# Scaling tokens by expert weights: a three-token load moved from behind the first input tile to behind the third, and one token's product moved from ScalarE to VectorE

## The chip, the core and the metric

The kernel runs on one core of a Trainium2 chip. The metric is the device time of one execution in microseconds (us). Before the change it is 240.13 us, the median of three runs that lie between 239.79 and 240.28 us.

## The reference, cut to what matters

```python
batch, seq, hidden, n_experts = 16, 1024, 512, 8
k = 2
x_expanded = x[:, :, np.newaxis, :].repeat(k, axis=2)
weights = expert_weights[..., np.newaxis]
return (x_expanded * weights).astype(np.float32)
```

Each of 16,384 tokens has a row of 512 float32 values and two weights. The output holds the row twice, each copy multiplied by one weight. The expert indices are not used. Input rows are 33.55 MB, the output is 67.11 MB, and the weights are 0.13 MB. There is no arithmetic beyond one multiplication per output value.

## The kernel before, in words

128 partitions hold 128 tokens each. They are cut into five **tiles** of 25 tokens per partition (`groups`, L32) and a rest of three (`LAST`, L34); 5 x 25 + 3 = 128. Within a tile the 25 rows of a partition lie one behind another in memory, so a tile's load is one row of 25 x 2 KB = 50 KB per partition.

- **Loads** are issued from ScalarE (its DMA queue is q10 in the profile). Two input tiles fit in memory at a time (`x_pool`, two buffers, L44). `load(i)` (L68) issues tile i; tile 0 is loaded in two steps of 9 and 16 tokens (`FIRST`, L35). Behind tile 0, still inside `load(0)`, stands the load of the last three tokens into a tile of its own, `z_tile` (L84 and L85). Tiles 0 and 1 are loaded at the start (L154); tile i + 2 is issued when tile i has been used up (L159), since it takes the same buffer. On ScalarE's queue the order is thus: tile 0 (9 tokens), tile 0 (16), the three tokens, tile 1, then tile 0's products on ScalarE, tile 2, and so on.
- **Weights** are loaded by SyncE (queue q1) in three pieces between the two steps of tile 0: those of tile 0 (L95), of tiles 1 to 4 (L97), and of the last three tokens (L104). A partition of each piece is 200 bytes (four times 200 for the middle piece) or 24 bytes long.
- **Products** go into one output ring, `o_ring`, that has room for one tile, 25 tokens of 1024 values (L48). Each tile is cut into chunks: two of 13 and 12 tokens for tiles 0 and 1, three of 9, 8 and 8 for the later tiles (L157). `SHARES` (L36) says how many tokens of a chunk VectorE computes: it takes them four at a time (L127, `CH` = 4), and ScalarE takes the remaining tokens of the chunk, two activations for each (L117). A chunk of a tile can be written to the ring only when the output transfer of the chunk that lay there before has landed.
- **Stores** are issued from SyncE, queue q1, one per chunk (L152), behind the weights on the same queue. The last one is the store of the three tokens, whose product VectorE makes in one instruction at the end (L160).

The framework puts in all waits on semaphores; the order of the instructions on each engine is that of the program.

Of the kernel before, what the change touches and what calls it, by code (L numbers as in the profile page):

```python
# [1 line left out]

# [4 lines left out]


@with_exitstack
def kernel(  # L10
    ctx: ExitStack,
    tc: tile.TileContext,
    x: bass.AP,
    expert_indices: bass.AP,
    expert_weights: bass.AP,
    out: bass.AP,
):
    nc = tc.nc

    batch, seq, hidden = x.shape  # L20
    k = expert_weights.shape[-1]
    P = nc.NUM_PARTITIONS
    ntok = batch * seq
    assert ntok % P == 0
    A_TOTAL = ntok // P

    f32 = mybir.dt.float32
    row = k * hidden
    CH = 4


    groups = [25, 25, 25, 25, 25]  # L32
    TX = max(groups)
    LAST = 3  # L34
    FIRST = [9, 16]  # L35
    SHARES = [[9, 8], [9, 8], [9, 8, 8]]  # L36
    assert sum(groups) + LAST == A_TOTAL

    xf = x.rearrange("b s h -> (b s) h")
    of = out.rearrange("b s k h -> (b s) (k h)")  # L40
    wf = expert_weights.rearrange("b s k -> (b s) k")

    w_pool = ctx.enter_context(tc.tile_pool(name="w_pool", bufs=1))
    x_pool = ctx.enter_context(tc.tile_pool(name="x_pool", bufs=2))  # L44
    o_pool = ctx.enter_context(tc.tile_pool(name="o_pool", bufs=1))

    w_tile = w_pool.tile([P, A_TOTAL * k], f32)
    o_ring = o_pool.tile([P, TX * row], f32)  # L48

    def rows(of_all, done, T):  # L50
        return of_all[done * P : (done + T) * P, :].rearrange(
            "(p a) n -> p (a n)", a=T
        )


    if LAST:
        z_pool = ctx.enter_context(tc.tile_pool(name="z_pool", bufs=1))
        z_tile = z_pool.tile([P, LAST * hidden], f32)

    tiles = []  # L60
    done = 0
    for n in groups:
        tiles.append((done, n))
        done += n

    loaded = []

    def load(i):  # L68
        if i >= len(tiles):
            return  # L70
        done, n = tiles[i]
        x_tile = x_pool.tile([P, TX * hidden], f32)
        src = rows(xf, done, n)
        steps = FIRST if i == 0 else [n]
        for e, step in enumerate(steps):
            at = sum(steps[:e])
            nc.scalar.dma_start(
                out=x_tile[:, at * hidden : (at + step) * hidden],
                in_=src[:, at * hidden : (at + step) * hidden],
            )  # L80
            if i == 0 and e == 0:
                for g in range(3):
                    weights(g)
        if i == 0 and LAST:  # L84
            nc.scalar.dma_start(out=z_tile, in_=rows(xf, A_TOTAL - LAST, LAST))  # L85
        loaded.append(x_tile)


    T0 = groups[0]
    G = len([n for n in groups[1:] if n == T0])  # L90
    head = (1 + G) * T0

    def weights(e):
        if e == 0:
            nc.sync.dma_start(out=w_tile[:, : T0 * k], in_=rows(wf, 0, T0))  # L95
        elif e == 1:
            nc.sync.dma_start(  # L97
                out=w_tile[:, T0 * k : head * k].rearrange("p (g n) -> p g n", g=G),
                in_=wf[T0 * P : head * P, :].rearrange(
                    "(g p a) n -> p g (a n)", g=G, p=P  # L100
                ),
            )
        else:
            nc.sync.dma_start(  # L104
                out=w_tile[:, head * k :], in_=rows(wf, head, A_TOTAL - head)
            )

    def product(engine, o_tile, t, x_in, c, m):

        o = t * row  # L110
        if engine is not None:
            for e in range(m * k):
                out_e = o_tile[:, o + e * hidden : o + (e + 1) * hidden]
                in_e = x_in[:, e // k * hidden : (e // k + 1) * hidden]
                w_e = w_tile[:, c + e : c + e + 1]
                if engine is nc.scalar or engine is nc.any and (c + e) % 3 == 2:
                    nc.scalar.mul(out=out_e, in_=in_e, mul=w_e)  # L117
                else:
                    nc.vector.tensor_scalar(
                        out=out_e,  # L120
                        in0=in_e,
                        scalar1=w_e,
                        scalar2=None,
                        op0=mybir.AluOpType.mult,
                    )
            return
        nc.vector.tensor_tensor(  # L127
            out=o_tile[:, o : o + m * row].rearrange(
                "p (t k h) -> p t k h", t=m, k=k
            ),  # L130
            in0=x_in[:, : m * hidden]
            .rearrange("p (t h) -> p t h", t=m)
            .unsqueeze(2)
            .to_broadcast([P, m, k, hidden]),
            in1=w_tile[:, c : c + m * k]
            .rearrange("p (t k) -> p t k", t=m)
            .unsqueeze(3)
            .to_broadcast([P, m, k, hidden]),
            op=mybir.AluOpType.mult,
        )  # L140

    def fill(o_tile, x_in, c, m, v):
        for t in range(0, v, CH):
            u = min(t + CH, v)
            product(None, o_tile, t, x_in[:, t * hidden : u * hidden], c + t * k, u - t)
        product(nc.scalar, o_tile, v, x_in[:, v * hidden :], c + v * k, m - v)

    def emit(src, dst, c, cuts, shares):
        for at, to, v in zip(cuts, cuts[1:], shares):
            o_tile = o_ring[:, at * row : to * row]  # L150
            fill(o_tile, src[:, at * hidden : to * hidden], c + at * k, to - at, v)
            nc.sync.dma_start(out=dst[:, at * row : to * row], in_=o_tile)  # L152

    for i in range(2):  # L154
        load(i)
    for i, (done, n) in enumerate(tiles):
        cuts = [0, 13, n] if i < 2 else [0, 9, 17, n]  # L157
        emit(loaded[i], rows(of, done, n), done * k, cuts, SHARES[min(i, 2)])
        load(i + 2)  # L159
    emit(  # L160
        z_tile,
        rows(of, A_TOTAL - LAST, LAST),
        (A_TOTAL - LAST) * k,
        [0, LAST],
        [LAST],
    )

# [1 line left out]
_INS = ['x', 'expert_indices', 'expert_weights']  # L169
_OUTS = [((16, 1024, 2, 512), 'float32')]  # L170


# [23 lines left out]
```

## Time and profile before

| what | value |
| --- | --- |
| median of three runs | 240.13 us (239.79 to 240.28) |
| the profiled execution: its time, its span | 240.12 us, 238.3 us |
| VectorE busy | 122.6 us, 51% of the span |
| ScalarE busy | 21.2 us, 9% of the span |
| bytes moved by DMA | 100.80 MB |

The span runs from the first to the last instruction that the profiler saw. The profiled execution's own time is 1.8 us longer than its span, and 0.01 us from the median. Every transfer is spread over 16 DMA engines, which work for both queues, q10 (loads) and q1 (weights and stores). A transfer consists of packets; here one packet is mostly one partition's row of the transfer.

### The profile page before, as it was taken

To read this page: it belongs to the slowest core of one execution; us is meant where nothing else is said; L and a number is where in the kernel's file an instruction comes from. 1 tells how busy PE (TensorE), PEld (TensorE's weight loads), DVE (VectorE), ACT (ScalarE), POOL (GpSimd) and SP (SyncE) were. 2 spreads that over 40 slices of the span, in tenths; PEclk is the share of its full clock that TensorE was granted. 3 is DMA by queue.
4 is the path that set the end of the run, shared out by engine and by line. 5 is a ranking of instruction groups with operands and counts; after the bars stand their busy time and mean duration, and the time that the engine had idled before them with its cause. 6 is when DMAs were issued, how large, how long until landed. Compare 5 with 4: busy or idle time off the path is not lost.

```text
span 238.3 us, 167 instructions
## 1 busy us (share of the span) xinstructions
DVE 122.6 (51%) x32; ACT 21.2 (9%) x33; POOL 0.2 (0%) x4
## 2 busy tenths in 40 slices
DVE  0599600000069292099405999493086999865000
ACT  0008900000061250000000000000000000000000
POOL 0000000000000000000000000000000000000000
DMA  7999999999999999999999999999999999999996
GB/s 264 465 386 504 457 414 413 413 424 429 429 396 429 472 465 426 422 404 405 412 484 431 402 434 444 414 434 425 449 408 461 434 440 431 421 413 423 440 434 264
DMA packets 3840, 100.80 MB, mean 423 GB/s; under 512 B 1152, under 2 KB 1152, under 8 KB 1280
## 3 DMA queue, kind: packets, MB, share of 16 engines
q1 hardware_dynamic: 2832, 67.24, 65.5%
q10 hardware_dynamic: 1008, 33.55, 33.2%
HBM read 33.69 MB, written 67.11 MB: 423 GB/s over the span
## 4 chain that ended last, share of the span: by engine, by line
DMA 58%; DVE 28%; issue 2%; another core or an unknown queue 2%; ACT 1%; DVEq 0%; SPq 0%
DMA out_dram<-o_ring 55%; DVE o_ring L127 28%; DMA x_tile<-in_x_dram 3%; ACT o_ring L117 1%; DVEq L127 0%; SPq L152 0%
## 5 line engine op out<-in xcount | busy, mean ns | idle before, releaser
L127 DVE TENSOR_TENSOR o_ring<-x_tile,w_tile 128x4096 f32<-128x4096 f32 (+1 forms) x31 | 119.3, 3905 | 93.2 <-DMA out_dram<-o_ring 82.3
L117 ACT ACTIVATE o_ring<-x_tile,w_tile 128x512 f32<-128x512 f32 x32 | 19.9, 708 | 47.1 <-DMA out_dram<-o_ring 47.0
L127 DVE TENSOR_TENSOR o_ring<-z_tile,w_tile 128x3072 f32<-128x3072 f32 x1 | 3.4, 3359 | 2.1 <-DMA out_dram<-o_ring 2.1
L117 ACT ACT_TABLE_LOAD x1 | 1.3, 1283 | 18.7 <-DMA x_tile<-in_x_dram 18.7
L180 POOL MEMSET const-uint8-127<- 128x1 uint8 x1 | 0.1, 102 | 0.0
L180 POOL MEMSET const-bfloat16-1.0<- 128x1 bf16 x1 | 0.1, 101 | 0.0
L180 POOL MEMSET const-float32-0.0<- 128x1 f32 x1 | 0.1, 98 | 0.2 <-issue 0.2
L180 POOL MEMSET const-float32-1.0<- 128x1 f32 x1 | 0.1, 98 | 0.0
## 6 DMA issues: line engine op xcount, KB each, us to landing
x_tile<-in_x_dram ACTq DMA_DIRECT2D x4, 6400.0 KB, 31.6
out_dram<-o_ring SPq DMA_DIRECT2D x6, 4096.0 KB, 21.5
out_dram<-o_ring SPq DMA_DIRECT2D x3, 4608.0 KB, 27.3
out_dram<-o_ring SPq DMA_DIRECT2D x2, 6656.0 KB, 33.1
out_dram<-o_ring SPq DMA_DIRECT2D x2, 6144.0 KB, 44.5
x_tile<-in_x_dram ACTq DMA_DIRECT2D x1, 4096.0 KB, 17.5
x_tile<-in_x_dram ACTq DMA_DIRECT2D x1, 2304.0 KB, 8.1
out_dram<-o_ring SPq DMA_DIRECT2D x1, 1536.0 KB, 19.5
```

What stands on the lines that cost most here:

```text
L117: nc.scalar.mul(out=out_e, in_=in_e, mul=w_e)
L127: nc.vector.tensor_tensor(out=o_tile[:, o : o + m * row].rearrange("p (t k h) -> p t k h", t=m, k=k), in0=x_in[:, : m * hidden] .rearrange ...
L180: nc = _bacc.Bacc("TRN2", target_bir_lowering=False, num_devices=1)
```

## The change

The changed kernel makes three edits.

- The load of `z_tile` is taken out of `load(0)` and put at the end of `load(2)`, behind the load of tile 2 on ScalarE's queue.
- Ahead of tile 2's load, ScalarE copies one element per partition from the very end of the output ring into `z_tile`. That element belongs to tile 0's last product on ScalarE, so the copy runs behind that product; and as the load of `z_tile` overwrites what the copy wrote, it waits for the copy.
- In tile 0's second chunk (12 tokens), VectorE computes nine tokens in place of eight, and ScalarE three in place of four. On VectorE this adds one instruction of 128 x 1024 values (as two groups of four and one token); on ScalarE it removes two activations of 128 x 512.

```diff
-    SHARES = [[9, 8], [9, 8], [9, 8, 8]]
+    SHARES = [[9, 9], [9, 8], [9, 8, 8]]
...
         x_tile = x_pool.tile([P, TX * hidden], f32)
         src = rows(xf, done, n)
         steps = FIRST if i == 0 else [n]
+        if i == 2 and LAST:
+            nc.scalar.copy(out=z_tile[:, :1], in_=o_ring[:, TX * row - 1 :])
         for e, step in enumerate(steps):
...
-        if i == 0 and LAST:
+        if i == 2 and LAST:
             nc.scalar.dma_start(out=z_tile, in_=rows(xf, A_TOTAL - LAST, LAST))
         loaded.append(x_tile)
```

The order on ScalarE is then: tile 0 (9 tokens), tile 0 (16), tile 1, 14 activations of tile 0, the copy, tile 2, the three tokens, tile 1's activations, and so on as before. Bytes, number of transfers and the order on SyncE are the same.

## The prediction

> **What bounds the kernel now.** I read the page first, for its engines and queues, and then the busy time by stretches.
>
> ```profile
> DVE 122.6 (51%) x32; ACT 21.2 (9%) x33; POOL 0.2 (0%) x4
> ...
> DMA  7999999999999999999999999999999999999996
> ...
> DMA packets 3840, 100.80 MB, mean 423 GB/s; under 512 B 1152, under 2 KB 1152, under 8 KB 1280
> ...
> q1 hardware_dynamic: 2832, 67.24, 65.5%
> q10 hardware_dynamic: 1008, 33.55, 33.2%
> ```
>
> The two queues' packets fill 65.5 + 33.2 = 98.7% of the time of 16 DMA engines. Only 1.3% of 238.3 us, 3.1 us, is idle. Where it lies, the stretches tell (DMA share and GB/s are the last two columns):
>
> ```profile
> 0.00:2.00 2.00, 0.00 (x0) 0.00 (x0) 0.20 (x4) 1.00 0.21 41
> 2.00:25.07 23.07, 16.24 (x5) 6.32 (x10) 0.00 (x0) 1.00 1.01 426
> 25.07:51.90 26.83, 2.38 (x1) 4.87 (x8) 0.00 (x0) 1.00 1.02 430
> 51.90:67.50 15.60, 0.00 (x0) 0.00 (x0) 0.00 (x0) 1.00 1.00 433
> 67.50:82.00 14.50, 9.90 (x3) 5.02 (x9) 0.00 (x0) 1.00 1.01 438
> 82.00:100.00 18.00, 8.76 (x2) 4.99 (x8) 0.00 (x0) 1.00 0.98 422
> 100.00:128.00 28.00, 14.30 (x5) 0.00 (x0) 0.00 (x0) 1.00 0.99 425
> 128.00:218.00 90.00, 71.05 (x18) 0.00 (x0) 0.00 (x0) 1.00 1.00 432
> 218.00:236.50 18.50, 0.00 (x0) 0.00 (x0) 0.00 (x0) 1.00 0.98 423
> 236.50:238.30 1.80, 0.00 (x0) 0.00 (x0) 0.00 (x0) 1.00 0.02 7
> ```
>
> The first 2 us miss 0.79 x 2.0 = 1.6 us and the last 1.8 us miss all but 2%, 1.76 us; together 3.3, so the whole idle time. (Shares over 1.00 come from packets counted whole in the stretch in which they start.) From 2.0 to 236.5 us no stretch lies below 0.98. **The bound is the transport of 100.80 MB**, and its rate hardly depends on what is moved: 426 and 430 GB/s for the loads at the start, 433 for stores alone.
>
> The chain of waits names VectorE for 28%, but that is only the partner in a ring: a product waits for a store to land, and the next store waits for the product, while the other chunk's store fills the engines.
>
> **What the change touches.** These are the first transfers, from the list of issues in narrow windows (the column after the size is us from issue to landing), with the instructions around them:
>
> ```profile
> z_tile<-in_x_dram ACTq DMA_DIRECT2D x1, 768.0 KB, 19.1
> x_tile<-in_x_dram ACTq DMA_DIRECT2D x1, 6400.0 KB, 33.8
> x_tile<-in_x_dram ACTq DMA_DIRECT2D x1, 6400.0 KB, 21.8
> w_tile<-in_expert_weights_dram SPq DMA_DIRECT2D x1, 100.0 KB, 36.7
> w_tile<-in_expert_weights_dram SPq DMA_DIRECT2D x1, 3.0 KB, 50.3
> 1.17 0.42 SPq L97 DMA_DIRECT2D w_tile<-in_expert_weights_dram  x1
> 1.64 0.50 SPq L104 DMA_DIRECT2D w_tile<-in_expert_weights_dram  x1
> 1.64 0.52 ACTq L85 DMA_DIRECT2D z_tile<-in_x_dram  x1
> 2.19 0.81 ACTq L77 DMA_DIRECT2D x_tile<-in_x_dram  x1
> 8.83 18.62 DVE L127 TENSOR_TENSOR o_ring<-x_tile,w_tile 128x4096 f32<-128x4096 f32 x5 [8.83 <-DMA x_tile<-in_x_dram]
> 20.03 9.91 ACT L117 ACTIVATE o_ring<-x_tile,w_tile 128x512 f32<-128x512 f32 x16
> 29.97 0.37 ACTq L77 DMA_DIRECT2D x_tile<-in_x_dram  x1
> 25.07 42.40 DMA out_dram<-o_ring
> ```
>
> So the three tokens land at 1.64 + 19.1 = 20.7 us, tile 1 at 36.0, tile 2 at 29.97 + 21.8 = 51.8, the middle weights at 37.9 and the last weights, 3 KB issued at 1.64, only at 51.9. The first store is issued at 25.07 and lands at 67.47, though its 6.82 MB (6656 KB) take only 15.7 us at 433 GB/s: it does not begin before some 51.8 us. Why a store should stand still for 26 us, the packets between 30 and 49 us show:
>
> ```profile
> q10 hardware_dynamic: 176, 8.19, 103.0%
> q1 hardware_dynamic: 176, 0.01, 0.7%
> ```
>
> Each queue gave 176 packets: the engines take **one packet of each queue in turn**. A weight packet is 200 or 24 bytes, a load packet 50 KB. While loads stand in q10, the weights in q1 advance by one packet for each load packet, and the first store stands behind the weights. Per engine (128 partitions / 16) the weights are 8 + 32 + 8 = 48 packets, and the five loads ahead of tile 3 are 5 x 8 = 40. So the opening is one burst of loads until about 51.8 us, and then stores alone.
>
> **The change, part by part.**
>
> *The load of the three tokens, 786 KB.* Its 8 packets per engine leave the place ahead of tile 1 and come behind tile 2, in the same burst. At 428 GB/s (the mean of the two rows from 2.00 to 51.90) they take 1.84 us. Tile 1 lands at 34.2, tile 2 at 50.0, the three tokens at 51.8, and the burst ends where it ended: the packets ahead of the first store are the same in number and size, and so are their turns with the weights. Term: 0. What comes early is waited for by nobody: VectorE and ScalarE take up tile 1 when the first store has landed, not when the tile has:
>
> ```profile
> 67.57 5.01 ACT L117 ACTIVATE o_ring<-x_tile,w_tile 128x512 f32<-128x512 f32 x8 [37.63 <-DMA out_dram<-o_ring]
> 67.59 9.90 DVE L127 TENSOR_TENSOR o_ring<-x_tile,w_tile 128x4096 f32<-128x4096 f32 x3 [40.13 <-DMA out_dram<-o_ring]
> 77.55 0.33 SPq L152 DMA_DIRECT2D out_dram<-o_ring  x1
> 214.61 3.36 DVE L127 TENSOR_TENSOR o_ring<-z_tile,w_tile 128x3072 f32<-128x3072 f32 x1 [2.11 <-DMA out_dram<-o_ring]
> ```
>
> What comes late has room: the middle weights lose eight turns and land near 50 us instead of 37.9, needed at 67.59; the three tokens land at 51.8, needed at 214.61. On q1 nothing changes its place.
>
> *The shares of tile 0.* VectorE gets one more 128x1024 instruction, ScalarE two activations less:
>
> ```profile
> L127 DVE TENSOR_TENSOR o_ring<-x_tile,w_tile 128x1024 f32<-128x1024 f32 x5 | 6.1, 1219 | 0.0
> L117 ACT ACTIVATE o_ring<-x_tile,w_tile 128x512 f32<-128x512 f32 x32 | 19.9, 708 | 47.1 <-DMA out_dram<-o_ring 47.0
> L180 POOL MEMSET const-float32-1.0<- 128x1 f32 x1 | 0.1, 98 | 0.0
> ```
>
> VectorE ends tile 0 at 8.83 + 18.62 + 1.22 = 28.7 us. ScalarE's 16 activations take 9.91 us, 0.62 each in a row; 14 take 8.67 and end at 28.7. The second store is issued at about 28.8 in place of 29.97, but it queues behind the first, which lands at 67.47. Term: 0.
>
> *The copy.* No row shows a one-element copy on ScalarE. Its bounds are 0.1 us (a 128x1 memset on GpSimd) and 0.71 us (an activation of 512 elements on ScalarE itself); by size it is nearest to the memset, by engine to the activation, and I take 0.3. It waits for the activation ahead of it, and behind it on ScalarE stand tile 2's load, the three tokens' load and tile 1's activations. Tile 2's load is thus issued at 29.0 (28.8 to 29.5), which is 1.0 us earlier than before (0.5 to 1.2), and the three tokens' load some 0.4 us behind it. q10 holds work until tile 1 has passed, at 34.2, so tile 2 is 5 us ahead of its turn: the copy is covered, and would cost only from about 5 us on. Term: 0.
>
> *The handover from loads to stores.* Before, the last load packet of each engine is 50 KB long (1.9 us at 27 GB/s, a sixteenth of 430); after, it is 6 KB (0.23 us). No row shows this handover with short packets. From below: if the change took away every loss in the opening, 2.00 to 51.90 would run at 433 GB/s, and that saves 23.07 x 7/433 + 26.83 x 3/433 = 0.56 us. From above: if the first store had to be fetched after the loads ended, as the very first load was, that costs the 1.6 us of the first row. The nearest row is that of the same short load inside the burst before, 2.00 to 25.07 with a share of 1.01: its eight short packets, between two long loads, left no hole. I take 0.
>
> *Sum.* 240.12 + 0 + 0 + 0 + 0 = 240.12 us for the profiled execution, and as this stands 0.01 us from the median, I forecast **240.1 us**: no change. 0.2%, 0.48 us, is about what a measurement of this kernel can tell from none.
>
> **The rivals.**
>
> *The handover gets shorter* (faster). A hole that long last packets cause goes when the last packets are short. It gives at most the 0.56 us above: 239.5 us. For it: the opening is the place with the lowest rate among the long read stretches, 426. Against it: 2.00 to 25.07, where most of that loss lies, does not change.
>
> *The handover gets longer* (slower). The fetch of the first store is hidden behind the load packets ahead of it, 1.9 us long before and eight of 0.23 us after, and a restart shows. The full price is 1.6 us: 241.7 us. It decides from about 0.5 us of uncovered fetch on. Against it stands the short load before, ahead of tile 1's first packet, with no hole. The Trainium skill, page "DMA: Bandwidth & Descriptors", section "Latency and other measured facts", gives about 0.6 us from issue to first byte on these queues; by that the rival would end at 240.7 us. The trace's first load shows more: the share of 0.21 in the first 2 us.
>
> *The read queue runs dry ahead of tile 2* (slower). It needs tile 2's issue at 34.2 us or later, so a copy of more than 5 us, or one that waits for a store. It would let the first store begin early and mix loads with stores, at the 422 to 425 GB/s of 82 to 128 us; for the 21.4 MB from 2 to 51.9 us moved at 422 in place of 428, 0.7 us: 240.8 us. The order on ScalarE speaks against it: the copy reads what ScalarE itself wrote just before.
>
> *The change does not do what it says*: the held-back load goes early all the same, or lands late but unneeded. Then it is 240.1 us too.
>
> **How the numbers follow.** Forecast, no change: 0.68 (239.7 to 240.5, the spread of the three runs, 0.25 us to either side, and some of the bounds). Not done as said, same time: 0.02. Shorter handover: 0.16. Longer handover: 0.10. Read queue dry: 0.04. So faster by over 0.2% 0.16, within 0.2% 0.70, slower 0.14. The range takes in the shorter handover and the lower part of the longer one, by half its price: 239.4 to 240.8; left out is most of the longer handover, about 1 in 10, and a little at either end.
>
> **What would show it.** Right: the burst of loads ends and the first store lands at 67.5 within 0.3 us; tile 2's load is issued near 29.0; the DMA share stays at 0.98 or more from 2 to 236.5; the middle weights land near 50 us. Wrong: a landing of the first store later or earlier by 0.5 us or more with the rest shifted along (a handover), a store's packets ahead of 49 us (the read queue dry), or a share below 0.98 in a stretch behind 67.5, which would mean a wait that I have not seen. What no term of mine covers is a change in the rate itself at equal work, as between 422 and 438 among the stretches.

## The result, and the profile after

The changed kernel takes 239.84 us, the median of 16 runs (239.57 to 240.09), beside 240.28 us for 16 runs of the kernel before. The ratio is 0.9981 with a 95% interval of 0.9972 to 0.9990: 0.44 us less, just inside what the prediction called no change. A ratio leaves out runs over 1.5% above the fastest of the same kernel, while a median takes in every run. Measured again later, the changed kernel gave 0.9990 (0.9978 to 1.0002) and, with a wider copy that delays only the three tokens' load, by 0.1 us, 0.9976 (0.9964 to 0.9988). All of its runs and those of the wider copy, 38 in number, lie between 239.49 and 240.28 us. Of 117 runs of the kernel before the fastest is as fast, 239.47, but 26 lie above 240.4, up to 241.13. The change takes away slow outliers more than it speeds up the best execution.

From the page of the changed kernel: the engines, the DMA packets and the two queues.

```profile
DVE 123.8 (52%) x33; ACT 20.2 (8%) x32; POOL 0.2 (0%) x4
...
DMA packets 3840, 100.80 MB, mean 424 GB/s; under 512 B 1152, under 2 KB 1152, under 8 KB 1280
...
q1 hardware_dynamic: 2832, 67.24, 65.7%
q10 hardware_dynamic: 1008, 33.55, 33.2%
```

The same bytes in the same packets fill 98.9% of a span of 237.9 us. VectorE has the one instruction more, ScalarE lost two activations and gained the copy. Busy time by stretches, DMA share and GB/s last:

```profile
2.00:25.07 23.07, 16.02 (x5) 6.08 (x9) 0.00 (x0) 1.00 1.00 425
25.07:51.90 26.83, 3.75 (x2) 4.07 (x8) 0.00 (x0) 1.00 1.03 429
51.90:67.50 15.60, 0.00 (x0) 0.00 (x0) 0.00 (x0) 1.00 1.00 434
67.50:82.00 14.50, 9.90 (x3) 5.01 (x8) 0.00 (x0) 1.00 1.01 438
82.00:100.00 18.00, 8.76 (x2) 5.01 (x8) 0.00 (x0) 1.00 0.97 422
100.00:128.00 28.00, 14.57 (x5) 0.00 (x0) 0.00 (x0) 1.00 0.98 423
128.00:218.00 90.00, 70.77 (x18) 0.00 (x0) 0.00 (x0) 1.00 1.00 433
218.00:236.50 18.50, 0.00 (x0) 0.00 (x0) 0.00 (x0) 1.00 0.98 423
```

No stretch moved by more than 2 GB/s: transport still bounds the kernel. The prediction named a share below 0.98 behind 67.5 us as a sign of a wait that it had not seen; 82 to 100 us now has 0.97, but it moves the same 422 GB/s as before. The instructions around the change, from the timeline, and the landings from the list of issues in narrow windows (tile 1, tile 2, the three tokens, the middle weights, the last weights):

```profile
1.63 0.52 ACTq L79 DMA_DIRECT2D x_tile<-in_x_dram  x1
9.05 19.77 DVE L129 TENSOR_TENSOR o_ring<-x_tile,w_tile 128x4096 f32<-128x4096 f32 x6 [9.05 <-DMA x_tile<-in_x_dram]
28.98 0.19 ACT L76 COPY z_tile<-o_ring 128x1 f32<-128x1 f32 x1
29.05 0.34 ACTq L79 DMA_DIRECT2D x_tile<-in_x_dram  x1
29.43 0.46 ACTq L87 DMA_DIRECT2D z_tile<-in_x_dram  x1
67.83 9.90 DVE L129 TENSOR_TENSOR o_ring<-x_tile,w_tile 128x4096 f32<-128x4096 f32 x3 [39.01 <-DMA out_dram<-o_ring]
127.66 22.90 DVE L129 TENSOR_TENSOR o_ring<-x_tile,w_tile 128x4096 f32<-128x4096 f32 x6 [11.69 <-DMA out_dram<-o_ring]
214.16 3.36 DVE L129 TENSOR_TENSOR o_ring<-z_tile,w_tile 128x3072 f32<-128x3072 f32 x1 [2.13 <-DMA out_dram<-o_ring]
```

```profile
x_tile<-in_x_dram ACTq DMA_DIRECT2D x1, 6400.0 KB, 32.6
x_tile<-in_x_dram ACTq DMA_DIRECT2D x1, 6400.0 KB, 20.4
z_tile<-in_x_dram ACTq DMA_DIRECT2D x1, 768.0 KB, 30.2
w_tile<-in_expert_weights_dram SPq DMA_DIRECT2D x1, 100.0 KB, 48.6
w_tile<-in_expert_weights_dram SPq DMA_DIRECT2D x1, 3.0 KB, 50.5
```

Tile 1 lands at 1.63 + 32.6 = 34.2 us, tile 2 at 49.5, the middle weights at 1.15 + 48.6 = 49.8 and the last ones at 52.1. The opening is the forecast one. The execution starts 0.22 us late (first product at 9.05 in place of 8.83), and tile 1's first product starts 0.24 us late (67.83 for 67.59): the handover from loads to stores costs the same. In these two executions the gain comes behind it. The first instruction that waits for the second chunk of tile 1 to be stored starts at 127.66; the same row of the kernel before:

```profile
127.93 22.90 DVE L127 TENSOR_TENSOR o_ring<-x_tile,w_tile 128x4096 f32<-128x4096 f32 x6 [12.15 <-DMA out_dram<-o_ring]
```

So 0.24 us late has become 0.27 us early, a gain of 0.5 us between 67 and 128 us, where tile 3's load takes turns with stores; at the last product it is 0.45 us (214.16 for 214.61). Two more profiles with the changed order of loads repeat this stretch, but not the total. From tile 1's first product to this row it is 59.83 us here, 59.78 in a second profile of the changed kernel and 59.75 with the wider copy, beside 60.34 and 60.55 in two profiles of the kernel before. Yet the execution of that second profile took 240.20 us.

At the end, one of 16 engines at work all through a window counts as 0.06 of the share, and a window counts a packet where it begins. The kernel before

```profile
236.00:236.50 0.50, 0.00 (x0) 0.00 (x0) 0.00 (x0) 1.00 0.42 172
236.50:237.00 0.50, 0.00 (x0) 0.00 (x0) 0.00 (x0) 1.00 0.06 25
```

has one engine that begins another packet past 236.5 us, and the changed kernel has none:

```profile
236.00:236.50 0.50, 0.00 (x0) 0.00 (x0) 0.00 (x0) 1.00 0.24 98
236.50:237.00 0.50, 0.00 (x0) 0.00 (x0) 0.00 (x0) 1.00 0.00 0
```

This is no mark of the change: the second profile of the changed kernel has a share of 0.12 there, two engines, and so has the second profile of the kernel before.

### The profile page after: what moved, and what is told of

Its sections match the earlier page's. It is cut to its first block, busy times and chain, and to the rows that moved or that the text cites. A ratio compares the mean times of both kernels' runs of the same rounds, so it can differ in the third digit from the quotient of the medians.

```text
span 237.9 us, 167 instructions
## 1 busy us (share of the span) xinstructions
DVE 123.8 (52%) x33; ACT 20.2 (8%) x32; POOL 0.2 (0%) x4
## 4 chain that ended last, share of the span: by engine, by line
DMA 68%; DVE 18%; ACT 3%; issue 2%; ACTq 0%; DVEq 0%; SPq 0%
DMA out_dram<-o_ring 60%; DVE o_ring L129 18%; DMA x_tile<-in_x_dram 7%; ACT o_ring L119 2%; ACT L119 1%; ACTq L79 0%; DVEq L129 0%; SPq L154 0%; ACTq L119 0%
## 5 line engine op out<-in xcount | busy, mean ns | idle before, releaser
L119 ACT ACTIVATE o_ring<-x_tile,w_tile 128x512 f32<-128x512 f32 x30 | 18.7, 708 | 48.1 <-DMA out_dram<-o_ring 48.0
## 6 DMA issues: line engine op xcount, KB each, us to landing
x_tile<-in_x_dram ACTq DMA_DIRECT2D x4, 6400.0 KB, 30.5
out_dram<-o_ring SPq DMA_DIRECT2D x2, 6656.0 KB, 33.1
```

## The experiments

Two things were open: which edit makes the small gain, and whether each edit is really worth nothing by itself. **Theory 1**: the place of the three tokens' load makes the gain, by short last packets at the handover. **Rival**: the share and the earlier issue of tile 2, or scatter. A third, the **theory of the lead**, arose from the first four experiments. Each edit is shown against the kernel that its heading names, the kernel before or the changed one.

**The kernel before, against itself.** No edit.

> The kernel before itself, run a second time as if it were a changed one. Every theory expects a ratio of 1.000; its interval tells how much of the 0.9981 of the changed kernel could be chance. If the median comes out 0.4 us or more from that of the kernel before, the theory that the difference is only scatter gains.

240.06 us (12 runs), ratio 1.0003 (0.9992 to 1.0014). So 0.1% either way is scatter.

**The new share alone, in the kernel before.**

```diff
-    SHARES = [[9, 8], [9, 8], [9, 8, 8]]
+    SHARES = [[9, 9], [9, 8], [9, 8, 8]]
```

> Only the share of tile 0's second chunk (nine tokens on VectorE in place of eight), the load of the three tokens stays behind tile 0. Theory 1 (the place of the three tokens' load, the last and short load ahead of the first store, makes the difference): no change against the kernel before, 240.2 to 240.4 us. Rival (tile 2 is issued 1 us earlier, and that makes it): 239.8 to 239.9 us, a ratio of 0.998.

239.92 us (11 runs, 239.69 to 240.64), ratio 1.0002 (0.9992 to 1.0012). By the ratio the share alone gives nothing.

**The changed kernel with the old share: only the moved load and the copy.**

```diff
-    SHARES = [[9, 9], [9, 8], [9, 8, 8]]
+    SHARES = [[9, 8], [9, 8], [9, 8, 8]]
```

> The load of the three tokens behind tile 2 with the one-element copy, but the old share (eight tokens on VectorE). Theory 1 (place of the load): 239.8 to 239.9 us, a ratio of 0.998. Rival (the share and the earlier issue of tile 2): 240.2 to 240.4 us, a ratio of 1.000.

243.97 us (6 runs, 241.07 to 245.74), ratio 1.0104 (1.0058 to 1.0150). Neither theory had this. Without the new share the move costs 1.0% by the ratio, and 1.6% by the medians (243.97 beside 240.12). The timeline of this kernel, and the packets of both queues between 30 and 48 us (count, MB, share):

```profile
30.03 0.19 ACT L76 COPY z_tile<-o_ring 128x1 f32<-128x1 f32 x1
30.09 0.34 ACTq L79 DMA_DIRECT2D x_tile<-in_x_dram  x1
```

```profile
q10 hardware_dynamic: 99, 4.25, 60.2%
q1 hardware_dynamic: 406, 3.13, 41.1%
```

In the changed kernel, the same window:

```profile
q10 hardware_dynamic: 160, 7.37, 95.0%
q1 hardware_dynamic: 166, 0.03, 0.9%
```

Tile 2's load is issued only 1.04 us later than in the changed kernel, 4.1 us ahead of the 34.2 us at which tile 1 lands there; and still it comes too late. The read queue is empty, the weights rush through, and 3.1 MB of the first store slip in among the loads: the rival "the read queue runs dry", with a point that decides between 29.05 and 30.09 us and not at 34.2.

The packets of tile 1 itself show the late load, too. Its 16 last packets, one on each engine, begin between 31.05 and 31.8 us in both kernels. These are the load packets that begin between 30.5 and 32.5 us, first in the changed kernel, then in this one:

```profile
q10 hardware_dynamic: 16, 0.82, 94.8%
q10 hardware_dynamic: 16, 0.82, 145.3%
```

Of a window of 2 us, 94.8% is 1.9 us for a packet, and 145.3% is 2.9 us. The packet that ought to hide the fetch of tile 2 is itself slower by 1 us; why, no run shows, and the DMA share does not tell, since a slow packet counts as busy. In the changed kernel these packets begin 2.0 us and more after tile 2's load is issued, here only 1.0 to 1.7 us after it.

At the end, this kernel has two engines (0.12) that go on when the others are done, and one of them (0.06) goes on still longer, past 240.5 us:

```profile
237.50:238.00 0.50, 0.00 (x0) 0.00 (x0) 0.00 (x0) 1.00 0.30 123
238.00:238.50 0.50, 0.00 (x0) 0.00 (x0) 0.00 (x0) 1.00 0.12 49
239.00:239.50 0.50, 0.00 (x0) 0.00 (x0) 0.00 (x0) 1.00 0.12 49
239.50:240.00 0.50, 0.00 (x0) 0.00 (x0) 0.00 (x0) 1.00 0.06 25
240.50:241.00 0.50, 0.00 (x0) 0.00 (x0) 0.00 (x0) 1.00 0.06 25
```

**The changed kernel without the copy.**

```diff
-        if i == 2 and LAST:
-            nc.scalar.copy(out=z_tile[:, :1], in_=o_ring[:, TX * row - 1 :])
```

> The changed kernel without the one-element copy. The framework then issues the three tokens' load ahead of tile 2's, so it lies in the middle of the burst of loads, and the last packets ahead of the first store are 50 KB long as before the change. Theory 1 (a short last load at the handover makes the difference): 240.2 to 240.4 us, as before the change. Rival (the three tokens' load only has to leave the head of the queue, ahead of tile 1): 239.8 to 239.9 us.

239.98 us (11 runs, 239.75 to 240.31), ratio 0.9990 (0.9981 to 0.9999): between the two, and not told apart. The timeline shows what the copy is for: without it the load is issued at 21.36 us, in the midst of tile 0's activations and ahead of tile 2's load.

From here on **the theory of the lead**: tile 2's load must be issued some 4 to 5 us ahead of its turn, or the first store gets among the loads. The expectations count the lead to the end of tile 1's packets, which they put at 33.5 to 34 us; below I count it to tile 1's landing, for which there are rows.

**The changed kernel again, and with a wider copy.** The second kernel copies 512 elements per partition.

```diff
-            nc.scalar.copy(out=z_tile[:, :1], in_=o_ring[:, TX * row - 1 :])
+            nc.scalar.copy(out=z_tile[:, :hidden], in_=o_ring[:, TX * row - hidden :])
```

> The changed kernel once more, beside the kernel before on the same chip, with more runs. Theory 1 (a small gain of its own, from the order of the loads): a ratio near 0.998 again, about 239.7 to 239.9 us. Rival (scatter): a ratio of 1.000, within the 0.1% that the kernel before showed against itself.

> The changed kernel with a copy of 512 elements per partition in place of one; it holds tile 2's load back by some 0.5 us more, so that it is issued at about 29.5 us, between the changed kernel (29.05, on time) and the kernel with the old share (30.09, 1% slower). Theory of the lead (tile 2's load must be issued some 4.5 us ahead of the end of tile 1's packets, or the first store slips in among the loads): at the edge, so between 239.8 and 244 us, and more scattered than the changed kernel; the packets of q1 between 30 and 48 us tell which way each went. Rival (the old share is slow for another reason, on VectorE or ScalarE): 239.8 to 239.9 us.

240.03 us and 239.72 us (11 runs each), ratios 0.9990 and 0.9976 as given above. The wider copy missed its purpose: it runs from 28.86 to 29.48 us, but tile 2's load is issued at 28.93, since that load does not wait for a copy into another tile. Only the three tokens' load moved, to 29.51.

**Tile 2 late in the kernel before.** Here the copies go into tile 2's own buffer, so that its load has to wait for them.

```diff
+        if i == 2:
+            for d in range(3):
+                nc.scalar.copy(
+                    out=x_tile[:, d * hidden : (d + 1) * hidden],
+                    in_=o_ring[:, TX * row - hidden :],
+                )
```

> The kernel before, its three tokens' load at its old place, with three copies of 512 elements into tile 2's buffer ahead of tile 2's load; they hold that load back by about 1.9 us, to 31.9 us, where tile 1's packets end at about 35.6. The lead is then 3.7 us, as short as in the kernel with the old share (30.09 against 34). Theory of the lead: 1% slower, 242 to 245 us, and some 3 MB on q1 between 30 and 48 us. Rival (only the moved short load, its late place or the copy's semaphore, makes the old share slow): 240.1 to 240.3 us, and 0.01 MB on q1.

241.67 us (12 runs, 240.10 to 244.70), ratio 1.0051 (1.0025 to 1.0076). The three tokens lie at their old place, the share is the old one, and the kernel is slow all the same once tile 2's load comes at 31.75 us, 4.3 us ahead of the 36.0 us at which tile 1 lands in the kernel before. The profiled execution, 240.26 us, is one of the faster; it has 1.08 MB of the store among the loads:

```profile
q10 hardware_dynamic: 140, 6.35, 84.1%
q1 hardware_dynamic: 198, 1.08, 14.3%
```

So part of the engines took the load in time and part did not. Tile 1's 16 last packets, which begin between 33.1 and 33.75 us, tell the same: of the 2 us from 32.5 they fill 105.4%, where all in time give 94.8% and all late gave 145.3%. That a late tile 2 slows the kernel is thus shown without the moved load and without the new share; the forecast of a full 1% was too high.

**The kernel before, with the weights on the other queue.**

```diff
-                for g in range(3):
-                    weights(g)
+                weights(0, nc.sync)
...
+        if i == 1:
+            for g in range(1, 3):
+                weights(g, nc.scalar)
...
-    def weights(e):
+    def weights(e, queue):
...
```

> The kernel before, with the weights of tiles 1 to 4 and of the last three tokens loaded on ScalarE's queue behind tile 1, so that nothing stands ahead of the first store on SyncE's queue but tile 0's weights. Both theories expect the first store to begin at about 26 us in place of 51 and to take turns with the loads of tiles 1 and 2. Theory of the mixture (loads and stores in turn move fewer bytes per second and drive the 16 engines apart): 242 to 245 us, as in the kernel with the old share. Rival (only the bytes count, whatever their order): 240.1 to 240.3 us.

241.21 us (9 runs, 240.77 to 241.82), ratio 1.0044 (1.0029 to 1.0059). The first store now lands 27.2 us after its issue in place of 42.4, and between 30 and 48 us

```profile
q1 hardware_dynamic: 109, 5.80, 74.5%
q10 hardware_dynamic: 96, 2.46, 31.7%
```

stores and loads share the engines. This shows that the weights at the head of q1 are what holds the first store back in the kernel before. The price is 0.4%, not 1%, but what it is made of is not shown, for the edit brings a second delay: the moved weights now land so late that tile 1's first product waits for them and not for the store:

```profile
67.76 18.57 DVE L129 TENSOR_TENSOR o_ring<-x_tile,w_tile 128x4096 f32<-128x4096 f32 x5 [40.19 <-DMA w_tile<-in_expert_weights_dram]
```

**The changed kernel with a late tile 2.**

```diff
-            nc.scalar.copy(out=z_tile[:, :1], in_=o_ring[:, TX * row - 1 :])
+            for d in range(2):
+                nc.scalar.copy(
+                    out=x_tile[:, d * hidden : (d + 1) * hidden],
+                    in_=o_ring[:, TX * row - hidden :],
+                )
+            nc.scalar.copy(out=z_tile[:, :1], in_=x_tile[:, 2 * hidden - 1 : 2 * hidden])
```

> The changed kernel, new share and all, but with two copies of 512 elements into tile 2's buffer ahead of tile 2's load, which must wait for them: issued at about 30.4 us in place of 29.05, a lead of 3.2 us ahead of the end of tile 1's packets (33.6) in place of 4.6. Theory of the lead (about 4 us are needed): 243 to 246 us, as with the old share (lead 3.4), and 2 to 3 MB on q1 between 30 and 48 us. Rival (the old share itself is what was slow, the lead only scatters): 239.7 to 240.5 us and 0.03 MB on q1.

Tile 2's load is issued at 30.18 us, 4.0 us ahead of 34.2. The 12 runs fall into two heaps: six from 239.75 to 240.12 us, six from 243.64 to 250.02. The ratio, 0.9997 (0.9978 to 1.0016), speaks of the first heap alone; the median of all 12 is 241.88. The profiled execution is of the first heap, at 239.75 us, and has the store fully among the loads:

```profile
q10 hardware_dynamic: 95, 4.04, 56.5%
q1 hardware_dynamic: 416, 3.45, 45.2%
```

So the new share does not protect from a store among the loads. Of the 12 runs with the lead gone, half lie 4 to 10 us above the other half, and none of the 38 runs with the lead in place does. A store among the loads need not cost anything, else this execution would be slow too; what makes one execution lose 4 us and another none is open, and there is no profile of the second heap.

**The changed kernel with the old share and the lead given back.** The three tokens are loaded twice, early and late.

```diff
-    SHARES = [[9, 9], [9, 8], [9, 8, 8]]
+    SHARES = [[9, 8], [9, 8], [9, 8, 8]]
...
-        if i == 2 and LAST:
+        if i in (0, 2) and LAST:
             nc.scalar.dma_start(out=z_tile, in_=rows(xf, A_TOTAL - LAST, LAST))
```

> The kernel with the old share and the moved load, but the three tokens are also loaded at the old place, behind tile 0, so that they are loaded twice: 0.79 MB more, which at 428 GB/s are 1.84 us, and tile 1's packets end 1.84 us later, near 35.5 us. Tile 2's load has a lead of 5.4 us again. Theory of the lead: the first store waits for the burst as in the changed kernel, and the time is 240.1 + 1.8 = 241.9 us (241.6 to 242.2). Rival (the old share itself): 244 + 1.8 = 245.8 us.

242.41 us (6 runs, 241.66 to 243.17), ratio 1.0101 (1.0081 to 1.0121): 2.3 us over the kernel before for 1.84 us of bytes, somewhat above the forecast 241.6 to 242.2, and far from 245.8. Tile 2's load, issued at 30.18 us as in the kernel just shown, is here 5.9 us ahead of tile 1's landing at 36.1, and no store slips in:

```profile
q10 hardware_dynamic: 160, 7.37, 94.9%
q1 hardware_dynamic: 160, 0.01, 0.7%
```

**The kernel before with the new share and short last packets, without the move.**

```diff
-    SHARES = [[9, 8], [9, 8], [9, 8, 8]]
+    SHARES = [[9, 9], [9, 8], [9, 8, 8]]
...
-        steps = FIRST if i == 0 else [n]
+        steps = FIRST if i == 0 else [n - LAST, LAST] if i == 2 else [n]
```

> The kernel before with the new share, the three tokens' load at its old place, and tile 2's load in two steps of 22 and 3 tokens, so that the last packets ahead of the first store are 6 KB long as in the changed kernel. The second step waits for the middle weights to land, near 38 us, which is 10 us ahead of its turn. Theory 1 (short last packets at the handover make the small gain): a ratio of 0.998, as in the changed kernel. Rival (the place of the three tokens' load, or scatter): 1.000, as with the new share alone.

239.92 us (11 runs, 239.70 to 240.21), ratio 0.9989 (0.9978 to 1.0000). It leans to theory 1 and does not settle it.

**The changed kernel with the three tokens ahead of tile 3.**

```diff
-        if i == 2 and LAST:
+        if i == 3 and LAST:
```

(at both places)

> The changed kernel with its copy and the three tokens' load put one tile later, directly ahead of tile 3's load, so that their packets take turns with stores. The burst at the start is 1.84 us shorter, and its last packets are 50 KB long. Theory 1 (short last packets at the handover make the gain): 240.1 us, 1.000. Rival (the three tokens only have to leave the head of the read queue): 0.998. Tile 2 is issued near 29 us with a lead of 4.6 us, so no store slips in.

241.16 us (12 runs; three up to 239.88, one at 240.57, eight from 241.09 to 241.37), ratio 1.0028 (1.0009 to 1.0046). Worse than either expected. Its profile has one engine that goes on beginning packets from 236.5 to 238 us, alone:

```profile
236.50:237.00 0.50, 0.00 (x0) 0.00 (x0) 0.00 (x0) 1.00 0.06 25
237.00:237.50 0.50, 0.00 (x0) 0.00 (x0) 0.00 (x0) 1.00 0.06 25
237.50:238.00 0.50, 0.00 (x0) 0.00 (x0) 0.00 (x0) 1.00 0.06 25
```

From 236.0 to 236.5 us its share, 0.36, is much like the 0.42 of the kernel before, so 15 engines end in time, and the one that fell behind accounts for the span of 239.3 us beside 238.3.

## Why the prediction came out as it did

- **The bound and the sum** held: the same bytes at the same rate, 240.1 us forecast, 239.84 measured. The forecast was no change; the loss that one might read into VectorE's 28% of the chain is not there, nor does VectorE's extra instruction show. That the whole came to nothing was luck in part: the move alone costs 1%, and only together with the new share is it free, by a margin that the prediction did not know.
- **One packet of each queue in turn, and the weights as the cork of q1**, held. The middle weights landed at 49.8 us (forecast 50), the last ones at 52.1 (51.9), and taking them off q1 freed the first store. (Of the 176 packets of q10 that the prediction counted, 8.19 MB make 160 packets of 50 KB; the other 16 are far smaller.) The three tokens landed at 59.6 us instead of 51.8: on at least one engine a packet of theirs came after the store had begun (in the second profile they landed at 52.3). Nobody waits for them until 214.
- **The copy** took 0.19 us (0.3 forecast), tile 2's load came at 29.05 (29.0).
- **The cover of that copy was mis-sized**, and with it the value of the share. The prediction had tile 2 "5 us ahead of its turn" and the copy free up to about 5 us. In fact 4.3 us ahead of tile 1's landing is partly late, 4.0 to 4.1 is late, and 5.2, the changed kernel's lead, is in time: less than 1 us of cover. The share, priced at nothing, is what pays for the move: moving the load out brings tile 1 forward by 1.8 us (36.0 to 34.2), and the share brings tile 2's issue forward by 1.0 to 1.1 us (30.09 and 30.18 to 29.05) to keep up. Without it: 1.0104.
- **The rival "read queue runs dry"** was right in its mechanism, and wrong in its point and its price: 3.9 us by the medians with the old share (2.5 by the ratio), forecast 0.7, which counted only the rate of mixed traffic. In the profile of 244.22 us, one engine that works alone past 240.5 us is part of what it left out.
- **The handover** neither shortened nor lengthened by more than 0.05 us in the profiled executions. The two rivals on it did not come true. The loss that the first one wanted to save is there all the same, hidden in a full DMA share, since a slow packet counts as busy. In the kernel before, tile 2's 16 last packets, which begin between 47.3 and 49.3 us, take 124.1% of 2 us, 2.5 us each in place of 1.9. The changed kernel pays it in its short packets: its loads that begin between 48.2 and 52 us, 0.77 MB, take 69.5% of 3.8 us, 2.6 us on each engine, where 27 GB/s would give 1.8.

```profile
q10 hardware_dynamic: 16, 0.82, 124.1%
q10 hardware_dynamic: 156, 0.77, 69.5%
```

- **The small gain** was no term of the sum. In the profiles it arises behind the handover, by 128 us, and in the runs it shows as fewer late outliers; how the place of a short load does that is open. The new share alone (1.0002) does not bring it; the load in the middle of the burst (0.9990), short last packets alone (0.9989) and the change itself (0.9981, 0.9990) cannot be told apart at this scatter. The stretch from tile 1's first product to the row near 128 us leans to the place of the load: the changed kernel takes 59.8 us, and so does the double load with the old share (59.79), while the new share alone takes 60.20, the load in the middle 60.12, short last packets 60.03 and the kernel before 60.34 and 60.55. These are one or two profiles of each.

## What to carry to other kernels

When 98% of DMA time is busy, moving a load gains next to nothing; the question is only whether a queue can run dry, and the margin to look for is the time from a load's issue to the end of the transfer ahead of it, here between 4.3 and 5.2 us and not zero. A full DMA share does not show that margin: a packet that takes 2.9 us in place of 1.9 counts as busy. An edit that looks worthless in the sum, such as one token's product moved to another engine, may be what keeps that margin: test each edit alone. When a tuned transport loop still scatters, look at its last microsecond for a single engine that is still at work.

## What the runs showed of the hardware that was not expected

- A load that was issued while the engines were busy needed a lead of over 4 us to follow the load ahead of it without a gap: on time at 5.2, 5.9 and 6.0 us ahead of that load's landing, partly late at 4.3, late at 4.1 and 4.0. Of this lead, 1.9 us are the last packet of 50 KB ahead of it. Counted to the beginning of that packet, 2.0 us and more was on time, 1.35 to 2.0 partly late, and 1.0 to 1.7 late. Whether shorter packets ask for a shorter lead no run shows. At the idle start, the first load was issued at 0.73 us and the first of its packets began within the window from 1.6 to 2.1 us.
- The last load packets before an engine turns to stores were slower: 2.5 us in the kernel before and 2.9 us with the late tile 2, in place of 1.9. The cause is open.
- The 16 DMA engines do not end together, and the last one sets the time: one engine, 0.06 of the share, went on alone for 1.5 us in the kernel with the three tokens ahead of tile 3.
- The same kernel with a short lead took 239.75 us in one execution and 250.02 in another. A store slipped in among the loads in the one of 239.75 us, which lost nothing by it; that the same store is what costs the slow ones up to 10 us is likely and not shown.
